# Three 256-column matmuls in the feed-forward part, and weight and activation tiles whose first byte lies at 64 modulo 128

## The chip, the core and the metric

The kernel runs on one core of a Trainium2 chip. The metric is the device time in microseconds (us) of one execution. The median of three runs of the kernel before is 1634.89 us (1634.41 to 1635.89).

The engines are called as the profile calls them: PE is TensorE (its matmuls; PEld are its weight loads), DVE is VectorE, ACT is ScalarE, POOL is GpSimd, SP is SyncE, which issues the DMAs. A matmul has a *stationary* operand of 128x128 values, brought in by a weight load, and a *moving* operand of up to 512 columns that streams past it; sums land in a PSUM bank of 512 f32 columns per partition.

## The reference, cut to what matters

The reference is two transformer-like blocks on 256 tokens of 2048 features, all in float32: a first block with chunk attention and a gated recurrence, a second one with pooling, latent attention, memory attention and a feed-forward part. The change of form touches the feed-forward part:

```python
def conv_glu_ffn(h, w_gate, w_up, conv_w, conv_b, w_down):
    S = h.shape[1]
    g = h @ w_gate                       # [256, 2048] @ [2048, 5632]
    gp = jnp.pad(g, ((0, 0), (CONV_WIDTH - 1, 0), (0, 0)))
    gc = conv_b
    for j in range(CONV_WIDTH):
        gc = gc + conv_w[j] * gp[:, j:j + S]
    return (jax.nn.silu(gc) * (h @ w_up)) @ w_down
```

## The kernel before

**How a product is made.** Every float32 weight product is made of three products of a shorter form (float32r): weights and activations are each split into a high and a low part, and high x high, high x low and low x high are summed in PSUM. `split_w` makes the parts of a half tile of weights (128 partitions x 1024 values): ACT rounds the raw tile `wr` into `wh` (L114), DVE subtracts to get `wl` (L115). `tile_mm` loads one weight tile of 1 MB by a DMA on SP's queue, splits it in two halves and emits the matmuls of each half. Its modes are: `N`, where the activations are stationary and 512 (or 384, or 320) columns of weights move; `T`, where a 128x128 block of weights is stationary and 256 tokens move, with three matmuls for each block (all at L162); and `T2`, for the feed-forward part alone, where the tile of activations holds high and low side by side, so that one matmul of 512 columns (L148) gives high x high and high x low at once, in the two halves of a bank, and one of 256 columns (L149) adds low x high to the first half.

**Stages.** The program runs, in this order: keys and values of the memory (mode N, activations in tiles named `s`), the input projection with modulation beside it (modes N and T, activations `h`), gates (T, `h`), output projection of block 1 (T, activations `yH` and `yL`), input projection of block 2 (N and T, `h`), latent attention (N), output projection of block 2 (T, `yH` and `yL`), and the feed-forward part: for each of 22 column pairs a gate matrix and an up matrix (T2, activations `h`), then 8 column groups of the down matrix (T2, activations `f`). The feed-forward part has 1408 pairs of matmuls on `h` and 704 on `f`.

**What sets the order.** The code is written out once and the order of each engine's queue is that of the code. Evictions are put on a queue of small closures (`later`), and `drain` emits some of them after each half tile, by the table BUDGET; AHEAD says by how many half tiles the splits go ahead of the products (one in gate and up, none in down). In the feed-forward part an eviction of the gate is, for each of two 128-feature blocks, a copy of the second half bank by ACT (L1283), an addition by DVE (L1284) and a product with the token factor by POOL (L1285), then the convolution (L1289 to L1291); of the up matrix a copy (L1311), an addition (L1312), a product (L1313) and a split (L119, L120); of the down matrix two additions (L1334, L1335) and a DMA of the result (L1337).

**Where tiles lie.** SBUF tiles are given out in the order of the code, pool by pool. Adding up their sizes gives these first bytes modulo 128: `wr`, `wh` and `wl` at 32; the tile of `h` at 0; the tiles `yH`, `yL`, `s` and `f` at 96. Steps inside these tiles are multiples of 512 bytes, so every operand of a matmul has the residue of its tile.

Of the kernel before, what the change touches and what calls it, by code (L numbers as in the profile page):

```python
# [26 lines left out]
# PSUM banks for the accumulation of weight products (the others serve everything else)  # L27
MM = 6
# by phase: half tiles by which the splits of the weights go ahead of their products,
# and how much waiting work (microseconds of VectorE) is emitted after each half tile  # L30
AHEAD = dict(mem=0, pass0=0, pass3=1, gz=0, az=1, out=0, in2=1, mla=1, o=0, ffn=1, down=0)
BUDGET = dict(mem=0.3, pass0=0.5, pass3=2.0, gz=1.3, az=1.1, out=0.5, in2=0.1, mla=0.9, o=0.6, ffn=0.1, down=0.3)
# which engine does each of a modulation tile's four chunks, VectorE or ScalarE with GpSimd:
# for the gate's column groups, and for the scale's and the shift's
GATES = ("VVVP", "VVVP", "VVVP", "VVVV")
PAIR = ("PPPP", "VVVV")
# where modulation tiles stand among the projection's column groups, and among the memory's weight tiles
# [3 lines left out]
# stages by which a recurrence pair's transposition follows its last level; costs of the recurrence's steps  # L41
# [17 lines left out]
def trunk_kernel(ctx, tc, a, out):  # L59
# [3 lines left out]
    const = ctx.enter_context(tc.tile_pool(name="const", bufs=1))  # L63
    wpool = ctx.enter_context(tc.tile_pool(name="w", bufs=2))
# [26 lines left out]
    def later(cost, fn, q=None):  # L91
        (bgq if q is None else q).append((cost, fn))

    def drain(budget):
        """Emits waiting work, of about budget microseconds on the vector engine."""
        while budget > 0 and (evq or bgq):
            cost, fn = (evq or bgq).popleft()
            fn()
            budget -= cost
# [24 lines left out]
    def submit(job):  # L124
        """Emits the products of half tiles AHEAD halves behind their splits."""
# [8 lines left out]
    def tile_mm(src, kc0, kt, cw, mode, banks, act, first, last, pre=None, post=None):  # L134
        """One weight tile [kt * P, cw]: banks += weights.T @ activations, transposed (T) or not (N), or transposed
        with a bank for each block, where the low parts of the activations have their own half (T2);
        pre comes before its products, post after them."""
# [4 lines left out]
        def one(kc, b, hi, lo):  # L142
            x = act(kc0 + kc)
            hi, lo = hi[:, kc % nk, :], lo[:, kc % nk, :]
            st, sp = first and kc == 0, last and kc == kt - 1
            if mode == "T2":
                s = slice(b * P, b * P + P)
                PE.matmul(banks[b], hi[:, s], x, start=st, stop=sp, skip_group_check=True)  # L148
                PE.matmul(banks[b][:, :T], lo[:, s], x[:, 0, :], start=False, stop=sp, skip_group_check=True)  # L149
                return  # L150
            xh, xl = x
# [1296 lines left out]
```

## Time and profile before

| what | value |
|---|---|
| median of three runs | 1634.89 us (1634.41 to 1635.89) |
| profiled execution, first to last instruction | 1632.6 us |
| granted clock of PE over the span | 0.993 |
| PE busy | 1569.8 us (96%), 9754 matmuls |
| DVE busy | 1155.7 us (71%) |
| ACT busy | 860.1 us (53%) |
| POOL busy | 378.4 us (23%) |
| moved from HBM | 328 MB, mean 202 GB/s |

The profile is of one execution. Its span lies 2.3 us under the median, which counts what lies ahead of the first instruction and behind the last. Matmuls overlap: the duration of one includes its way through the array, so the time that a stream of them takes is read from the distance of their starts, not from their durations. The view "chain that ended last" follows the run back from its end; a piece such as "2.74 PE mm L162 x24" says that 24 matmuls in a row took 2.74 us of it.

### The profile page before, as it was taken

What the parts mean: (1) busy time and instruction counts of PE and PEld (TensorE: products, weight loads), DVE (VectorE), ACT (ScalarE), POOL (GpSimd) and SP (SyncE); (2) the same over time, 40 slices, a digit from 0 to 9 for tenths busy, and PEclk for the clock granted to TensorE, in tenths of its full rate; (3) what the DMA queues carried; (4) which work ended last, traced back from release to release, by engine and by line L of the source; (5) the groups of instructions that cost most, each with busy time, mean ns of one, the idle gap of its engine ahead of it and who ended that gap; (6) DMA issues with size and microseconds to landing.
All of it is one profiled execution on the core that took longest, in us unless ns stands there. A gap on an engine that the chain in (4) does not pass through costs nothing.

```text
span 1632.6 us, 24896 instructions
## 1 busy us (share of the span) xinstructions
PE 1569.8 (96%) x9754; PEld 1398.2 (86%) x9754; DVE 1155.7 (71%) x1610; ACT 860.1 (53%) x1254; POOL 378.4 (23%) x363
## 2 busy tenths in 40 slices
PE   5789999999899999999999999999999999999999
PEld 4677888978899999888999888888888888888887
DVE  7876998899997778568676666666666666445444
ACT  6466555564556745467455555554555555333332
POOL 3523434056643112513002111111111111000000
PEclk9999999999999999999999999999999999999999
DMA  9568877544665486443445555555555555556553
GB/s 386 224 229 309 329 296 303 181 155 156 214 218 207 155 301 225 160 158 135 147 155 174 188 181 181 186 194 188 181 183 190 192 183 181 187 192 208 193 178 126
DMA packets 50949, 331.75 MB, mean 203 GB/s; under 512 B 5648, under 2 KB 8080, under 8 KB 13456
## 3 DMA queue, kind: packets, MB, share of 16 engines
q1 hardware_dynamic: 50832, 330.17, 56.6%
q8 instruction: 76, 1.25, 0.3%
q14 instruction: 41, 0.34, 0.1%
HBM read 328.05 MB, written 2.10 MB: 202 GB/s over the span
## 4 chain that ended last, share of the span: by engine, by line
PE 83%; DVE 9%; POOL 2%; issue 2%; DMA 2%; ACT 2%; SPq 0%; DVEq 0%; ACTq 0%; POOLq 0%
PE mm L162 32%; PE mm L148 30%; PE mm L149 15%; DVE wl L115 4%; DVE acc L374 1%; PE ax L716 1%; DMA wr<-in_w_mem_kv_dram 1%; ACT wh L114 1%; POOL acc L380 1%; PE ax L389 1%; DMA wr<-in_w_ada_dram 1%; PE ax L250 1%; PE ax L514 1%; DMA yH<-in_w_ada_dram 1%; PE ax L220 0%
## 5 line engine op out<-in xcount | busy, mean ns | idle before, releaser
L115 DVE TENSOR_TENSOR wl<-wr,wh 128x1024 fp32r<-128x1024 f32 (+2 forms) x516 | 666.0, 1293 | 372.3 <-PE mm L149 248.2
L114 ACT CAST wh<-wr 128x1024 fp32r<-128x1024 f32 (+2 forms) x516 | 534.5, 1039 | 493.9 <-PE mm L148 242.0
L148 PE MATMUL mm<-h,wh 128*128 128x512 f32 x1408 | 497.7, 397 | 0.0
L149 PE MATMUL mm<-h,wl 128*128 128x256 f32 x1408 | 396.9, 282 | 0.0
L148 PEld LDWEIGHTS mm<-h,wh 128*128 128x128 f32 x1408 | 264.4, 188 | 64.8
L149 PEld LDWEIGHTS mm<-h,wl 128*128 128x128 f32 x1408 | 266.2, 189 | 0.0
L148 PE MATMUL mm<-f,wh 128*128 128x512 f32 x704 | 248.8, 398 | 0.0
L162 PE MATMUL mm<-wh,h 128*128 128x512 f32 (+1 forms) x704 | 222.4, 391 | 0.0
L162 PE MATMUL mm<-h,wh 128*128 128x256 f32 x1152 | 212.6, 286 | 0.6 <-ACT wh L114 0.6
L149 PE MATMUL mm<-f,wl 128*128 128x256 f32 x704 | 198.1, 281 | 0.0
L162 PEld LDWEIGHTS mm<-h,wh 128*128 128x128 f32 x1152 | 179.6, 191 | 1.6 <-ACT wh L114 1.2
L162 PE MATMUL mm<-h,wl 128*128 128x256 f32 x576 | 164.5, 286 | 7.8 <-DVE wl L115 7.8
L148 PEld LDWEIGHTS mm<-f,wh 128*128 128x128 f32 x704 | 132.6, 188 | 32.7
L162 PEld LDWEIGHTS mm<-wh,h 128*128 128x128 f32 x704 | 131.1, 188 | 27.7
L162 PE MATMUL mm<-wl,h 128*128 128x512 f32 (+1 forms) x352 | 137.1, 389 | 3.3 <-DVE wl L115 3.2
L149 PEld LDWEIGHTS mm<-f,wl 128*128 128x128 f32 x704 | 132.3, 188 | 0.0
L162 PEld LDWEIGHTS mm<-h,wl 128*128 128x128 f32 x576 | 110.1, 191 | 9.9 <-DVE wl L115 9.8
L162 PE MATMUL mm<-yH,wh 128*128 128x256 f32 x512 | 117.5, 282 | 0.0
L162 PE MATMUL mm<-yL,wh 128*128 128x256 f32 x512 | 116.9, 280 | 0.0
L1285 POOL TENSOR_TENSOR gp<-sg,R 128x256 f32<-128x256 f32 x44 | 35.9, 818 | 326.8 <-DVE sg L1284 326.8
L162 PE MATMUL mm<-yH,wl 128*128 128x256 f32 x384 | 106.5, 279 | 2.7 <-DVE wl L115 2.7
L380 POOL TENSOR_TENSOR acc<-acc,pts 128x512 f32<-128x512 f32 x45 | 75.5, 1678 | 112.0 <-ACT pts L379 109.8
(315 smaller groups left out, 2030.1 us busy)
## 6 DMA issues: line engine op xcount, KB each, us to landing
wr<-in_w_in_dram SPq DMA_DIRECT2D x76, 1024.0 KB, 4.9
wr<-in_w_gate_dram SPq DMA_DIRECT2D x44, 1024.0 KB, 4.8
wr<-in_w_up_dram SPq DMA_DIRECT2D x44, 1024.0 KB, 4.9
wr<-in_w_down_dram SPq DMA_DIRECT2D x40, 1024.0 KB, 5.0
yH<-in_w_ada_dram SPq DMA_DIRECT2D x28, 1024.0 KB, 7.1
wr<-in_w_ada_dram SPq DMA_DIRECT2D x16, 1024.0 KB, 5.0
wr<-in_w_out_dram SPq DMA_DIRECT2D x16, 1024.0 KB, 4.9
wr<-in_w_o_dram SPq DMA_DIRECT2D x16, 1024.0 KB, 4.8
```

The source lines that it names most:

```text
L114: S.copy(hi, raw[:, k : k + n, :])
L115: V.tensor_tensor(lo, raw[:, k : k + n, :], hi.bitcast(F32), ALU.subtract)
L148: PE.matmul(banks[b], hi[:, s], x, start=st, stop=sp, skip_group_check=True)
L149: PE.matmul(banks[b][:, :T], lo[:, s], x[:, 0, :], start=False, stop=sp, skip_group_check=True)
L162: PE.matmul(o, l, r, start=st and i == 0, stop=sp and i == 2, skip_group_check=True)
L250: PE.transpose(ps[:, j * T + tb * P : j * T + tb * P + P], d[:, j, tb * P : tb * P + P], ident)
L374: V.scalar_tensor_tensor(accs[0], raw[:, k, :], cc, accs[0], ALU.mult, ALU.add)
L380: G.tensor_tensor(accs[1], accs[1], t, ALU.add)
L389: PE.matmul(ps[:, j * P : j * P + P], acc[:, j * P : j * P + P], ones, start=i == 0, stop=i == len(accs) - 1, skip_group_check=True)
L514: PE.matmul(po[:, :T], vblk(0), t[:, :T], start=True, stop=False, skip_group_check=True)
L716: PE.matmul(ps[:, j, b, :], k2[:, j, s], q2[:, j, s], start=True, stop=True)
L1285: G.tensor_tensor(gp[:, 2:], s, R3, ALU.mult)
```

## The change

In the feed-forward part mode `T2` gives way to mode `T`: three matmuls of 256 columns with 256 columns of output, both blocks of a column pair side by side in one bank. So the evictions work on 512 columns at a time and need no addition of half banks: the gate's is one DVE product with the token factor, straight from PSUM; the up matrix's one DVE product and a split; the down matrix's one DVE addition. Four small tiles of 32 bytes are put ahead of the tiles of four pools (`const`, `h`, `y` and `f`), which moves the first bytes of `wr`, `wh`, `wl`, `h`, `yH`, `yL`, `s` and `f` to 64 modulo 128. The matrices, the DMAs of weights, the splits of weights and the orders of everything else stay.

```diff
@@ trunk_kernel @@
     const = ctx.enter_context(tc.tile_pool(name="const", bufs=1))
+    const.tile([P, 8], F32, tag="pad0", name="pad0")
...
+    hpool.tile([P, 8], F32, tag="pad1", name="pad1")
...
     yp = by.enter_context(tc.tile_pool(name="y", bufs=1))
+    yp.tile([P, 8], F32, tag="pad2", name="pad2")
@@ tile_mm @@
-            x = act(kc0 + kc)
+            xh, xl = act(kc0 + kc)
             hi, lo = hi[:, kc % nk, :], lo[:, kc % nk, :]
             st, sp = first and kc == 0, last and kc == kt - 1
-            if mode == "T2":
-                s = slice(b * P, b * P + P)
-                PE.matmul(banks[b], hi[:, s], x, start=st, stop=sp, skip_group_check=True)
-                PE.matmul(banks[b][:, :T], lo[:, s], x[:, 0, :], start=False, stop=sp, skip_group_check=True)
-                return
-            xh, xl = x
             if mode == "T":
                 o = banks[b // 2][:, (b % 2) * T : (b % 2) * T + T]
                 s = slice(b * P, b * P + P)
                 trip = ((hi[:, s], xh), (hi[:, s], xl), (lo[:, s], xh))
@@ feed-forward @@
         fp = ctx.enter_context(tc.tile_pool(name="f", bufs=1))
+        fp.tile([P, 8], F32, tag="pad2", name="pad2")
...
-    act3 = lambda kc: h3[2][:, :, kc, :]
+    act3 = lambda kc: (h3[0][:, kc, :], h3[1][:, kc, :])
...
-        def start(k, b, gp):
-            G.memset(gp[:, 0:2], 0.0)
-            s = sg[0][:, k, :]
-            S.copy(s, b[:, T:])
-            V.tensor_tensor(s, b[:, :T], s, ALU.add)
-            G.tensor_tensor(gp[:, 2:], s, R3, ALU.mult)
+        def start(b, gp):
+            G.memset(gp[:, :, 0:2], 0.0)
+            V.tensor_tensor(gp[:, :, 2:], two(b), bc(R3, 2), ALU.mult)
...
-            for k, b in enumerate(banks):
-                later(0.4, lambda k=k, b=b: start(k, b, gp[:, k, :]), evq)
+            later(0.8, lambda: start(banks[0], gp), evq)
...
-        def one(k, b):
-            t = tmp([P, T], "ub")
-            S.copy(t, b[:, T:])
-            V.tensor_tensor(t, b[:, :T], t, ALU.add)
-            V.tensor_tensor(t, t, sg[0][:, k, :], ALU.mult)
-            split(t, f[j][:, 0, k, :], f[j][:, 1, k, :])
+        def one(b):
+            t = tmp([P, 2, T], "ub")
+            V.tensor_tensor(t, two(b), sg[0], ALU.mult)
+            split(t, f[j][:, 0], f[j][:, 1])
...
-        linear([(lambda kg: a["w_gate"][j, kg], 256, "T2", ev_gate(j, sg))], range(2), act3, kt=8,
+        linear([(lambda kg: a["w_gate"][j, kg], 256, "T", ev_gate(j, sg))], range(2), act3, kt=8,
                need=lambda kg, j=j: need3(j, kg))
-        linear([(lambda kg: a["w_up"][j, kg], 256, "T2", ev_up(j, sg))], range(2), act3, kt=8)
+        linear([(lambda kg: a["w_up"][j, kg], 256, "T", ev_up(j, sg))], range(2), act3, kt=8)
...
-    actf = lambda kc: f[kc // 2][:, :, kc % 2, :]
+    actf = lambda kc: (f[kc // 2][:, 0, kc % 2, :], f[kc // 2][:, 1, kc % 2, :])
...
-            V.tensor_tensor(x1[:, c, :], b[:, T:], x1[:, c, :], ALU.add)
-            V.tensor_tensor(x1[:, c, :], b[:, :T], x1[:, c, :], ALU.add)
-            if k:
-                SP.dma_start(out[:, c - 1 : c + 1, :], x1[:, c - 1 : c + 1, :])
+            V.tensor_tensor(x1[:, c, :], two(b), x1[:, c, :], ALU.add)
+            SP.dma_start(out[:, c, :], x1[:, c, :])
```

What moves is shown at two places. The first is PE's queue in the feed-forward part, in a gate or up tile on `h3`: before, a bank for each of the two blocks of weights, and two matmuls for each block and chunk.

```order
L149 MATMUL mm_10080<-h3_8453,wl_10104 128x256
L148 MATMUL mm_10079<-h3_8453,wh_10103 128x512
L149 MATMUL mm_10079<-h3_8453,wl_10104 128x256
L148 MATMUL mm_10080<-h3_8453,wh_10103 128x512
L149 MATMUL mm_10080<-h3_8453,wl_10104 128x256
```

The same place after ("x2" is two in a row of the same form: high x high and high x low); the last two rows are those of the next tile, in the next bank.

```order
L156 MATMUL mm_10379<-h3_8456,wl_10467 128x256
L156 MATMUL mm_10379<-h3_8456,wh_10466 128x256 x2
L156 MATMUL mm_10379<-h3_8456,wl_10467 128x256
L156 MATMUL mm_10502<-h3_8456,wh_10498 128x256 x2
L156 MATMUL mm_10502<-h3_8456,wl_10499 128x256
```

Two matmuls of 512 and 256 columns have become three of 256, and one bank takes what two took. The second place is DVE's queue in the feed-forward part, from one gate eviction to the end of the up matrix's: before, additions from PSUM (`mm`) for each block.

```order
L1284 TENSOR_TENSOR sg<-mm,sg 128x256
L1290 SCALAR_TENSOR_TENSOR sg<-gp,cols,sg 128x256
L1291 SCALAR_TENSOR_TENSOR sg<-gp,cols,sg 128x256
L1290 SCALAR_TENSOR_TENSOR sg<-gp,cols,sg 128x256
L115 TENSOR_TENSOR wl<-wr,wh 128x1024
L1291 SCALAR_TENSOR_TENSOR sg<-gp,cols,sg 128x256
L115 TENSOR_TENSOR wl<-wr,wh 128x1024 x2
L1312 TENSOR_TENSOR ub<-mm,ub 128x256
L1313 TENSOR_TENSOR ub<-ub,sg 128x256
L115 TENSOR_TENSOR wl<-wr,wh 128x1024
L120 TENSOR_TENSOR f_8942<-ub,f_8942 128x256
```

The same place after.

```order
L1280 TENSOR_TENSOR gp<-mm,R_8813 128x2x256
L116 TENSOR_TENSOR wl<-wr,wh 128x1024
L1285 SCALAR_TENSOR_TENSOR sg<-gp,cols,sg 128x256 x2
L1286 SCALAR_TENSOR_TENSOR sg<-gp,cols,sg 128x256
L116 TENSOR_TENSOR wl<-wr,wh 128x1024
L1286 SCALAR_TENSOR_TENSOR sg<-gp,cols,sg 128x256
L116 TENSOR_TENSOR wl<-wr,wh 128x1024 x2
L1305 TENSOR_TENSOR ub<-mm,sg 128x512
L116 TENSOR_TENSOR wl<-wr,wh 128x1024
L121 TENSOR_TENSOR f_8981<-ub,f_8981 128x512
```

The token factor's product has come from POOL to DVE, the additions are gone, and the weight splits stand between fewer and longer operations.

## Rows read from the trace of the kernel before

**Rows 1.** The page: span; busy us of each engine (share) xinstructions.

```profile
span 1632.6 us, 24896 instructions
PE 1569.8 (96%) x9754; PEld 1398.2 (86%) x9754; DVE 1155.7 (71%) x1610; ACT 860.1 (53%) x1254; POOL 378.4 (23%) x363
```

**Rows 2.** Busy us by stretches of the feed-forward part: gate and up, then down.

```profile
core 0: us, PE busy (x) PEld busy (x) DVE busy (x) ACT busy (x) POOL busy (x), PEclk, DMA share, GB/s
900.00:1370.00 470.00, 470.00 (x2662) 408.58 (x2661) 311.95 (x415) 245.31 (x355) 78.42 (x100) 1.00 0.53 186
1380.00:1620.00 240.00, 240.00 (x1361) 208.41 (x1360) 116.83 (x117) 90.34 (x88) 0.00 (x0) 1.00 0.56 188
```

**Rows 3.** Chain that ended last: start us, us, what; mode T on `h`.

```profile
419.01 2.84 PE mm L162 x24
511.43 11.36 PE mm L162 x96
```

**Rows 4.** The same chain: mode T on `yH` and `yL`, both output projections.

```profile
538.30 2.73 PE mm L162 x24
578.93 26.21 PE mm L162 x231
...
771.95 5.46 PE mm L162 x48
...
781.58 2.83 PE mm L162 x24
...
817.71 2.83 PE mm L162 x24
...
840.16 21.43 PE mm L162 x188
866.16 14.16 PE mm L162 x118
```

**Rows 5.** The same chain, gate and up: pieces of mode T2 on `h`.

```profile
900.03 0.24 PE mm L148
900.27 0.12 PE mm L149
900.39 0.23 PE mm L148
900.62 0.12 PE mm L149
```

**Rows 6.** Timeline of PE, mode N, 512 columns of weights moving: activations `s`, then `h`.

```profile
55.21 0.39 PE L162 MATMUL mm<-wl,s 128*128 128x512 f32 x1
...
57.95 0.39 PE L162 MATMUL mm<-wl,s 128*128 128x512 f32 x1
...
279.87 0.40 PE L162 MATMUL mm<-wl,h 128*128 128x512 f32 x1
...
282.67 0.40 PE L162 MATMUL mm<-wl,h 128*128 128x512 f32 x1
```

**Rows 7.** Groups of instructions: line engine op, names, shapes, count, busy us, mean ns.

```profile
L162 PE MATMUL mm<-h,wl 128*128 128x256 f32 x576 | 164.5, 286 | 7.8 <-DVE wl L115 7.8
L162 PE MATMUL mm<-wh,h 128*128 128x512 f32 x640 | 206.9, 398 | 0.0
L162 PE MATMUL mm<-wl,h 128*128 128x512 f32 x320 | 127.2, 398 | 3.3 <-DVE wl L115 3.2
```

**Rows 8.** The same view: evictions of the feed-forward part, and one of 512 columns (L1233).

```profile
L1284 DVE TENSOR_TENSOR sg<-mm,sg 128x256 f32<-128x256 f32 x44 | 18.3, 417 | 11.5 <-ACT sg L1283 11.5
L1285 POOL TENSOR_TENSOR gp<-sg,R 128x256 f32<-128x256 f32 x44 | 35.9, 818 | 326.8 <-DVE sg L1284 326.8
L1312 DVE TENSOR_TENSOR ub<-mm,ub 128x256 f32<-128x256 f32 x44 | 18.5, 421 | 11.8 <-ACT ub L1311 11.8
L1313 DVE TENSOR_TENSOR ub<-ub,sg 128x256 f32<-128x256 f32 x44 | 18.7, 426 | 3.0
L1233 DVE TENSOR_TENSOR x<-mm,x 128x512 f32<-128x512 f32 x8 | 5.5, 684 | 0.3
```

**Rows 9.** Timeline of the end.

```profile
1628.30 0.28 PE L149 MATMUL mm<-f,wl 128*128 128x256 f32 x1
...
1628.62 0.42 DVE L1334 TENSOR_TENSOR x<-mm,x 128x256 f32<-128x256 f32 x1 [0.53 <-PE mm L149]
1629.08 0.42 DVE L1335 TENSOR_TENSOR x<-mm,x 128x256 f32<-128x256 f32 x1
1629.53 0.34 SPq L1337 DMA_DIRECT2D out_dram<-x  x1
```

More of the change, by code (lines that the diff above doesn't have):

```diff
@@ L1308, in ev_up @@
     def ev_up(j, sg):
-        def one(k, b):
-            t = tmp([P, T], "ub")
-            S.copy(t, b[:, T:])
-            V.tensor_tensor(t, b[:, :T], t, ALU.add)
-            V.tensor_tensor(t, t, sg[0][:, k, :], ALU.mult)
-            split(t, f[j][:, 0, k, :], f[j][:, 1, k, :])
+        def one(b):
+            t = tmp([P, 2, T], "ub")
+            V.tensor_tensor(t, two(b), sg[0], ALU.mult)
+            split(t, f[j][:, 0], f[j][:, 1])
         def ev(banks):
-            for k, b in enumerate(banks):
-                later(1.0, lambda k=k, b=b: one(k, b), evq)
+            later(1.2, lambda: one(banks[0]), evq)
         return ev
@@ L1322, in trunk_kernel, with one @@
         sg = []
-        linear([(lambda kg: a["w_gate"][j, kg], 256, "T2", ev_gate(j, sg))], range(2), act3, kt=8,
+        linear([(lambda kg: a["w_gate"][j, kg], 256, "T", ev_gate(j, sg))], range(2), act3, kt=8,
                need=lambda kg, j=j: need3(j, kg))
-        linear([(lambda kg: a["w_up"][j, kg], 256, "T2", ev_up(j, sg))], range(2), act3, kt=8)
+        linear([(lambda kg: a["w_up"][j, kg], 256, "T", ev_up(j, sg))], range(2), act3, kt=8)
     finish()
     flush()
-    actf = lambda kc: f[kc // 2][:, :, kc % 2, :]
+    actf = lambda kc: (f[kc // 2][:, 0, kc % 2, :], f[kc // 2][:, 1, kc % 2, :])
     def ev_out(g):
-        def one(k, b):
-            c = 2 * g + k
-            V.tensor_tensor(x1[:, c, :], b[:, T:], x1[:, c, :], ALU.add)
-            V.tensor_tensor(x1[:, c, :], b[:, :T], x1[:, c, :], ALU.add)
-            if k:
-                SP.dma_start(out[:, c - 1 : c + 1, :], x1[:, c - 1 : c + 1, :])
+        def one(b):
+            c = slice(2 * g, 2 * g + 2)
+            V.tensor_tensor(x1[:, c, :], two(b), x1[:, c, :], ALU.add)
+            SP.dma_start(out[:, c, :], x1[:, c, :])
         def ev(banks):
-            for k, b in enumerate(banks):
-                later(0.8, lambda k=k, b=b: one(k, b), evq)
+            later(0.8, lambda: one(banks[0]), evq)
         return ev
@@ L1345, in trunk_kernel @@
     for g in range(8):
-        linear([(lambda kg: a["w_down"][g][:, 2 * kg : min(2 * kg + 2, FC // 4)], 256, "T2", ev_out(g))], range((FC + 7) // 8),
+        linear([(lambda kg: a["w_down"][g][:, 2 * kg : min(2 * kg + 2, FC // 4)], 256, "T", ev_out(g))], range((FC + 7) // 8),
                actf, kt=8, nkc=FC)
```

## The prediction

> **What bounds the kernel now.** I read the page first. PE is busy for 1569.8 of 1632.6 us, DVE for 71% of the span, ACT for 53% [rows 1]. So what counts is how long PE's stream takes, and where PE waits. Then I cut out the feed-forward part: in both stretches PE is busy for the whole window, 470 of 470 us and 240 of 240 us, while DVE has 312 and 117 us of work, ACT 245 and 90, and the DMAs use 53 to 56% of their engines [rows 2]. Nothing but PE sets the end there. The window of 470 us holds 2662 matmuls, or 1331 pairs: 470 / 1331 = 0.3531 us for a pair of 512 and 256 columns; the one of 240 us gives 240 / 680.5 = 0.3527 us. The part has 1408 + 704 = 2112 pairs, so 2112 x 0.353 = 746 us of the run, and every nanosecond on the cost of 768 columns is worth 2.1 us.
>
> What do 768 columns cost elsewhere, in the form that the change brings? The chain shows mode T in two speeds. On `h`, 96 matmuls take 11.36 us, so three take 11.36 / 32 = 0.3550 us, and 24 in another place take the same 0.355 [rows 3]. On `yH` and `yL` it is 26.21 x 3 / 231 = 0.3404 us in the first output projection (and 2.73 / 8 = 0.341 a little earlier), but in the second one 0.341 at 772 us, 2.83 / 8 = 0.354 from 781 to 836 us, 0.342 from 840 us, and 14.16 x 3 / 118 = 0.360 from 866 us [rows 4]. At the clock of these stretches (granted 1.00, which is 2.4 GHz [rows 2]) 768 columns are 0.320 us, so all forms lose something for each column: 0.020 us in the good speed, 0.035 in the middling one, 0.040 in the worst. The loss is not one for each matmul: a pair at 0.3531 loses about what a triple on `h` loses. It shows inside the gate too, where the chain gives 0.24 and 0.23 us by turns to the matmuls of 512 columns [rows 5]: 0.24 against the 0.213 of 512 columns at 2.4 GHz.
>
> What do the speeds go with? The tiles' first bytes modulo 128 are 32 for weights, 0 for `h`, 96 for `yH`, `yL`, `s` and `f`. In mode T the fast stretches have a moving tile at 96 against weights at 32: equal modulo 64. The tile `h` at 0 is not equal to 32 modulo 64, and no piece on it is fast. Mode N says the same the other way round: 12 matmuls of 512 columns take 57.95 - 55.21 = 2.74 us with `s` stationary (96 against 32), 0.2283 each, and 282.67 - 279.87 = 2.80 us with `h` (0 against 32), 0.2333 each [rows 6]. Against it stand the slow stretches of the second output projection, on the same residues, and mode T2 on `f`, at 96 too, with 0.3527. So equal residues modulo 64 look needed for the fast speed, and not sufficient. After the change all of these tiles lie at 64: equal modulo 64 everywhere, but also equal modulo 128, which no stretch of this trace has.
>
> **The change part by part.**
>
> *Pairs to triples, in the fast speed.* 2112 x (0.3404 - 0.3531) = -26.8 us. All of it lies on the path, since PE is never idle there. In the middling speed it is 2112 x (0.3550 - 0.3531) = +4.0 us, in the worst 2112 x (0.360 - 0.3531) = +14.6 us. These are the ends; I take the fast one, because both forms of evidence (modes T and N) are faster where residues are equal modulo 64, and the change makes them so.
>
> *Padding, other stages.* There are 576 triples of mode T on `h` [rows 7]: 576 x (0.3404 - 0.3550) = -8.4 us. Mode N has 640 + 320 = 960 matmuls with `h` [rows 7]: 960 x (0.2283 - 0.2333) = -4.8 us. In those stages DVE and POOL stand on the chain between the matmuls, so part of it turns into longer waits of PE for `wl`; I count half, -4.2 and -2.4 us.
>
> *Evictions.* For a column pair DVE loses two additions of the gate, two of the up matrix and two products (417, 421 and 426 ns), and gets one product and one from PSUM of 512 columns; the nearest row is 684 ns [rows 8]. That is 2.53 us against 1.37. ACT loses its copies, POOL its two products of 818 ns. None of this is on the path as long as DVE has work for two thirds of the time; if that cover were gone the same change would be a gain, not a loss. One bank takes what two took, so PE finds banks free earlier; it does not wait for banks now. The weight splits are not touched.
>
> *The end.* Behind the last matmul two additions of 0.42 us run from 1628.62 to 1629.50 us, then the DMA [rows 9]. One of 0.684 us [rows 8] stands in their place: -0.2 us.
>
> *Transfers.* Weights come by the same DMAs at 186 GB/s [rows 2]; at the fast speed they would have to come 4% faster, with DMA engines busy for a little over half. A raw tile that starts 32 bytes further costs between nothing and what 53% leaves free; I take nothing.
>
> The sum: -26.8 - 4.2 - 2.4 - 0.2 = -33.6 us on a span of 1632.6. The span is 2.3 us below the median; I keep that distance, so 1634.9 - 33.6 = 1601, rounded to 1602 us.
>
> **The rivals.**
>
> *Only the number of matmuls counts, not the padding (slower).* Then a triple costs what it costs on `h` now, 0.355 against 0.3531, in gate, up and down: 2112 x 0.0019 = +4.0 us, -0.2 at the end, 1638.7 us. For it: the pair and the triple are close, whatever the tile, and the second output projection changes its speed with no change of tile. Against it: mode N differs by tile. The Trainium skill, TensorE: Matmul & The Clock Gate, section Back-to-back issue gap, has a time of N / 2.4 + 2.5 ns for one matmul behind another, so three cost one 2.5 ns more than two, 2112 x 2.5 ns = 5.3 us by its figure (an estimate from that page); the trace agrees that the triple on `h` is dearer, with 1.9 ns, but not with the page's total of 0.3275 us for a triple, which no piece reaches.
>
> *Only down gains.* Gate and up stay at the speed of `h`, 1408 x 0.0019 = +2.7 us, and down goes to that of the first output projection, 704 x (0.3404 - 0.3527) = -8.7 us: 1628.7 us. Between this and the forecast lie mixtures such as the second output projection's, fast and slow by turns, around 1618 us.
>
> *Equal residues modulo 128 collide (slower).* Weight loads and moving columns are read at the same time; in the fast stretches they lie 64 bytes apart, in the slow ones on `h` 32 apart, after the change 0 apart. If it is distance that helps, zero is the worst: the 0.360 of the last piece [rows 4] everywhere, which is also what 0.24 for 512 columns makes of 768 [rows 5]. Feed-forward +14.6, mode T on `h` 576 x 0.005 = 2.9, mode N 960 x (0.240 - 0.2333) = 6.4, half of these two, together 19 us: 1654 us. It decides from the point where a triple costs 0.356 us, because 2112 x 0.003 = 6.3 us eat up what the other stages could still gain. For it: distance 64 is the only one with fast stretches. Against it: T2 on `f` has distance 64 as well and is slow. The Trainium skill, SBUF — State Buffer, section Who interferes with whom, gives PE two separate read ports, one for the moving operand and one for the weight load, so by it there is no such collision; the trace has weight loads beside every matmul at 0.3404 and at 0.360 alike, so it doesn't tell.
>
> **How the numbers follow.** Forecast 0.40 at 1602; only down, with the mixtures, 0.13 at 1618 to 1629; only the number counts, 0.20 at 1639; collision 0.27 at 1654. A difference under 0.2% (3.3 us) can't be told from no change. The forecast and nearly all of the second case are faster by more than that: 0.52. Of the third case half falls within it (0.10 with what is left of the second), the other half and the fourth are slower: 0.38. The range: the forecast's own spread runs from 1592 (the halves that I left out of the other stages, and a triple slightly under 0.3404) to 1615; to hold 8 in 10 it must reach through the third case and half of the fourth, to 1652. Below 1592 I leave 0.05, above 1652 0.14.
>
> **What the profile would show.** In the forecast the chain has triples of 0.340 in gate, up and down, 2.74 us for 24 matmuls in the stages on `h`, and 512 columns at 0.228 in mode N. If the padding does nothing, stages on `h` stay at 2.84 us for 24. In a collision, these stages get slower together with the feed-forward part: 24 matmuls at 2.88. The number of DVE's operations falls by 183 rows and its busy time in gate and up by about 22 x 1.2 = 26 us in every case; the end shortens by 0.2 us. The forecast would be wrong at its root if the two speeds of mode T have another cause than where tiles lie, such as a state that PE falls into and keeps; the second output projection is the sign of that.

## The result and the profile after

The changed kernel takes 1652.8 us (median of 4 executions, 1651.21 to 1658.08), the kernel before 1635.39 us beside it (1634.41 to 1637.15): a ratio of 1.0105, 95% interval 1.0088 to 1.0122. It is slower by 1.05%, where 1602 us had been forecast. The profiled execution of it is the one of 1658.08 us, with a span of 1656.2 us.

The page of the changed kernel, span and busy time of each engine (against [rows 1]):

```profile
span 1656.2 us, 28877 instructions
PE 1594.0 (96%) x11866; PEld 1524.5 (92%) x11866; DVE 1121.1 (68%) x1476; ACT 833.0 (50%) x1144; POOL 320.4 (19%) x297
```

PE has 2112 more matmuls and 24.2 us more busy time; DVE, ACT and POOL all have less. So the time lies in PE's stream, not in an engine that feeds it. The same two stretches of the feed-forward part, shifted by 25 us (against [rows 2]):

```profile
core 0: us, PE busy (x) PEld busy (x) DVE busy (x) ACT busy (x) POOL busy (x), PEclk, DMA share, GB/s
925.00:1395.00 470.00, 470.00 (x3919) 470.00 (x3919) 281.63 (x309) 216.02 (x246) 29.14 (x40) 1.00 0.51 183
1405.00:1645.00 240.00, 240.00 (x2002) 240.00 (x2002) 106.83 (x91) 88.35 (x84) 0.00 (x0) 1.00 0.53 184
```

PE is again busy all the time at the same granted clock of 1.00, which is 2.4 GHz. But 470 us hold 3919 matmuls, 1306.3 triples, so 768 columns take 470 x 3 / 3919 = 0.3598 us in gate and up and 240 x 3 / 2002 = 0.3596 us in down; a pair took 0.3531 and 0.3527. PEld, which loads the weights, went from 87% to 100%: there are three loads for 768 columns where there were two. Pieces of the chain that ended last, against [rows 3 and 4] (start us, us, what):

```profile
292.04 10.90 PE mm L156 x48
...
410.62 2.88 PE mm L156 x24
...
513.20 11.51 PE mm L156 x96
...
582.62 20.52 PE mm L156 x171
...
702.98 3.52 PE mm L156 x24
...
710.42 8.22 PE mm L156 x36
...
848.80 23.05 PE mm L156 x192
...
903.75 748.80 PE mm L156 x6240
```

One price stands in all pieces of mode T, whatever the stage: 11.51 / 96 = 0.1199 us for a matmul of 256 columns on `h`, 20.52 / 171 = 0.1200 and 23.05 / 192 = 0.1200 on `yH` and `yL`, and 748.80 / 6240 = 0.1200 in the piece that covers nearly all of the feed-forward part. Before, the stretches on `yH` and `yL` had 0.1135 (26.21 / 231), 0.1140 and, in places, 0.118. The pieces at 292, 703 and 710 us are mode N, with 320 columns (3.52 / 24 = 0.1467) and 512 columns (10.90 / 48 = 0.2271, 8.22 / 36 = 0.2283). 512 columns are faster than before, where they took 0.2333 on `h` [rows 6]; 320 columns are not, the chain before has 3.52 us for 24 as well.

Where did the 23.6 us between the two profiled spans come from? The first matmul of the part on `h`, and the first of down, in the timeline of the kernel before:

```profile
880.16 0.40 PE L148 MATMUL mm<-h,wh 128*128 128x512 f32 x1
...
1379.69 0.39 PE L148 MATMUL mm<-f,wh 128*128 128x512 f32 x1
```

and of the changed one, with its end (against [rows 9]):

```profile
889.85 0.40 PE L156 MATMUL mm<-h,wh 128*128 128x256 f32 x2
...
1398.94 0.40 PE L156 MATMUL mm<-f,wh 128*128 128x256 f32 x2
...
1652.26 0.28 PE L156 MATMUL mm<-f,wl 128*128 128x256 f32 x1
1652.58 0.69 DVE L1325 TENSOR_TENSOR x<-mm,x 128x512 f32<-128x512 f32 x1 [4.47 <-PE mm L156]
1653.29 0.34 SPq L1326 DMA_DIRECT2D out_dram<-x  x1
```

Ahead of the feed-forward part 889.85 - 880.16 = +9.7 us; gate and up 509.1 against 499.5 us, +9.6; down (to DVE's last eviction) 253.6 against 248.9, +4.7; behind that -0.4. The two middle terms are the triple's price: 1408 x (0.3598 - 0.3531) = 9.4 and 704 x (0.3596 - 0.3527) = 4.9. The first term is partly this execution's own: it is 5.3 us above the median of its kernel, and t_all32 below, which has the same distances between all tiles, begins its long piece 3.4 us earlier (900.34 against 903.75). The rest of it was not taken apart.

The evictions did what the diff says (against [rows 8]: four kinds of work on 256 columns became two on 512):

```profile
L1280 DVE TENSOR_TENSOR gp<-mm,R 128x512 f32<-128x512 f32 x22 | 15.2, 692 | 33.6 <-PE mm L156 33.6
L1305 DVE TENSOR_TENSOR ub<-mm,sg 128x512 f32<-128x512 f32 x22 | 15.2, 692 | 36.4 <-PE mm L156 36.4
```

Both wait for PE, not PE for them. This saving, some 30 us of DVE in the first stretch (311.95 against 281.63), is worth nothing here, where PE is busy all the time.

### The profile page after: what moved, and what is told of

The parts are those of the page before. It is cut to its first block, busy times and chain, and to the rows that moved or that the text cites. A ratio compares the mean times of both kernels' runs of the same rounds, so it can differ in the third digit from the quotient of the medians.

```text
span 1656.2 us, 28877 instructions
## 1 busy us (share of the span) xinstructions
PE 1594.0 (96%) x11866; PEld 1524.5 (92%) x11866; DVE 1121.1 (68%) x1476; ACT 833.0 (50%) x1144; POOL 320.4 (19%) x297
## 4 chain that ended last, share of the span: by engine, by line
PE 83%; DVE 8%; DMA 2%; POOL 2%; ACT 2%; issue 2%; SPq 0%; DVEq 0%; ACTq 0%; POOLq 0%
PE mm L156 78%; DVE wl L116 3%; DVE acc L371 1%; PE ax L713 1%; ACT wh L115 1%; DMA wr<-in_w_mem_kv_dram 1%; POOL acc L377 1%; PE ax L214 1%; PE ax L244 1%; DMA yH<-in_w_ada_dram 1%; PE ax L511 1%; PE ax L386 1%; DMA wr<-in_w_out_dram 0%; DVE yH L714 0%; PE ax L503 0%
## 5 line engine op out<-in xcount | busy, mean ns | idle before, releaser
L116 DVE TENSOR_TENSOR wl<-wr,wh 128x1024 fp32r<-128x1024 f32 (+2 forms) x516 | 679.2, 1318 | 381.6 <-PE mm L156 336.2
L156 PE MATMUL mm<-h,wh 128*128 128x256 f32 x3968 | 721.9, 285 | 0.4 <-ACT wh L115 0.4
L156 PEld LDWEIGHTS mm<-h,wh 128*128 128x128 f32 x3968 | 621.3, 193 | 1.4 <-ACT wh L115 1.0
L156 PEld LDWEIGHTS mm<-h,wl 128*128 128x128 f32 x1984 | 381.9, 193 | 9.7 <-DVE wl L116 9.4
L156 PE MATMUL mm<-f,wh 128*128 128x256 f32 x1408 | 253.5, 283 | 0.0
L156 PEld LDWEIGHTS mm<-f,wh 128*128 128x128 f32 x1408 | 219.8, 192 | 0.0
L156 PEld LDWEIGHTS mm<-wh,h 128*128 128x128 f32 x704 | 131.2, 188 | 24.2
L156 PEld LDWEIGHTS mm<-yH,wh 128*128 128x128 f32 x512 | 89.5, 193 | 2.4 <-ACT wh L115 2.4
L156 PEld LDWEIGHTS mm<-yL,wh 128*128 128x128 f32 x512 | 89.4, 193 | 0.0
L156 PEld LDWEIGHTS mm<-wl,h 128*128 128x128 f32 x352 | 66.2, 188 | 18.6 <-DVE wl L116 6.9
L156 PEld LDWEIGHTS mm<-yH,wl 128*128 128x128 f32 x384 | 74.0, 193 | 1.4 <-DVE wl L116 1.4
```

Source lines behind the costliest of these rows:

```text
L116: V.tensor_tensor(lo, raw[:, k : k + n, :], hi.bitcast(F32), ALU.subtract)
L156: PE.matmul(o, l, r, start=st and i == 0, stop=sp and i == 2, skip_group_check=True)
```

## The experiments

The change has two halves, so the first two runs make one each. After that the subject is where tiles lie. The places below are first bytes modulo 256, from the built programs; every tile steps by multiples of 512 bytes, so the place holds for all of its slices. d is the place of the activation tile less that of the weight tile, modulo 256. Before: weights at 32, `h` at 0 (d = 224), `y` tiles and `f` at 224 (d = 192). After: all at 64, d = 0. A run's name gives places modulo 128, as the prediction used them. All runs have the triples (mode T) except pair_at_64. The others differ from the changed kernel in pad tiles alone, but for the edits of `spread` that two of the later sections show. Where only one execution was timed, the text says "one execution".

**t_unpadded: the triples without the padding.**

```
-    const.tile([P, 8], F32, tag="pad0", name="pad0")
-    hpool.tile([P, 8], F32, tag="pad1", name="pad1")
-    yp.tile([P, 8], F32, tag="pad2", name="pad2")
-        fp.tile([P, 8], F32, tag="pad2", name="pad2")
```

> The change of form alone: three 256-column matmuls in the feed-forward part, without the padding (weights at 32 modulo 128, h at 0, yH, yL and f at 96). Theory 'distance' (what counts is the distance modulo 128 between the moving and the stationary tile: 0 is worst, 64 best, 32 between): gate and up keep 0.355 us for a triple (distance 32), down gets 0.340 to 0.354 (distance 64), and the stages before the feed-forward part stay as they are: 1629 to 1638 us. Rival 'form' (the three matmuls themselves cost the 0.360, the padding nothing): 0.360 everywhere in the feed-forward part, 1650 us.

1627.88 us (1625.86 to 1629.49), a ratio of 0.9945, interval 0.9928 to 0.9962: faster than before. Two windows inside gate and up, and inside down:

```profile
925.00:1370.00 445.00, 445.00 (x3763) 445.00 (x3762) 270.93 (x292) 206.28 (x234) 26.88 (x38) 1.00 0.53 185
1410.00:1600.00 190.00, 190.00 (x1679) 190.00 (x1678) 89.54 (x78) 73.47 (x70) 0.00 (x0) 1.00 0.60 208
```

A triple takes 445 x 3 / 3763 = 0.3548 us on `h`, and 190 x 3 / 1679 = 0.3395 us on `f`. This is the prediction's case "only down gains" (1628.7 us), by its own two prices. So the form alone is a gain.

**pair_at_64: the padding without the triples** (the kernel before with the pads).

```
+    const.tile([P, 8], F32, tag="pad0", name="pad0")
+    hpool.tile([P, 8], F32, tag="pad1", name="pad1")
+    yp.tile([P, 8], F32, tag="pad2", name="pad2")
+        fp.tile([P, 8], F32, tag="pad3", name="pad3")
```

> The padding alone: the pair of 512 and 256 columns stays, all weight and activation tiles at 64 modulo 128 (distance 0). Theory 'distance': the stages in mode T before the feed-forward part have 0.360 for a triple as in the changed kernel, and the pair in the feed-forward part goes to 0.24 + 0.12 = 0.360 as well: about 1652 us. Rival 'triples only' (distance 0 hurts only where a weight load runs beside every 256 columns): the pair stays at 0.353 or goes down towards 0.227 + 0.120 = 0.347, and the run ends between 1625 and 1640 us.

1624.4 us (1623.01 to 1626.55), a ratio of 0.9929, interval 0.9906 to 0.9953. The padding alone is a gain too. The first of the same windows:

```profile
925.00:1370.00 445.00, 445.00 (x2569) 392.36 (x2569) 303.06 (x401) 237.84 (x342) 74.05 (x99) 1.00 0.54 189
```

A pair takes 445 x 2 / 2569 = 0.3464 us against 0.3531, as the rival of the expectation has it. So the two halves gain 0.55% and 0.7% alone and lose 1.05% together. That is no sum of two effects, and one price accounts for it: with d = 0 every matmul, whatever its columns, loses the same 13 ns over its columns at 2.4 GHz. 256 columns: 0.1200 - 0.1067 = 13.3 ns. 320: 0.1467 - 0.1333 = 13.4 ns. 512: 0.2271 - 0.2133 = 13.8 ns (15.0 in the dearest of the three pieces). A pair is 320 + 2 x 13.2 ns, a triple 320 + 3 x 13.3 = 360 ns. At the places of before a pair lost 33 ns and a triple on `h` 35 ns: about the same, so the number of matmuls did not show. The padding made the loss one for each matmul, which helps whoever has few and long ones (mode N and T2) and hurts mode T; the other half of the change turned two matmuls into three.

**t_w64_h0_y32_f96 and t_w0_h0_y64_f32: different places for each tile.** Weights, `h`, `y`, `f` at 64, 128, 160, 96 (d = 64, 96, 32) and at 128, 128, 192, 160 (d = 0, 64, 32).

```
# t_w64_h0_y32_f96
-    hpool.tile([P, 8], F32, tag="pad1", name="pad1")
+    hpool.tile([P, 24], F32, tag="pad1", name="pad1")
-    yp.tile([P, 8], F32, tag="pad2", name="pad2")
+    yp.tile([P, 16], F32, tag="pad2", name="pad2")
-        fp.tile([P, 8], F32, tag="pad2", name="pad2")
# t_w0_h0_y64_f32
-    const.tile([P, 8], F32, tag="pad0", name="pad0")
+    const.tile([P, 24], F32, tag="pad0", name="pad0")
-    yp.tile([P, 8], F32, tag="pad2", name="pad2")
+    yp.tile([P, 24], F32, tag="pad2", name="pad2")
-        fp.tile([P, 8], F32, tag="pad2", name="pad2")
+        fp.tile([P, 16], F32, tag="pad3", name="pad3")
```

> Triples, weights at 64 modulo 128, h at 0 (distance 64), yH, yL and s at 32 (distance 32 below), f at 96 (distance 32 above). Theory 'distance': triples on h, so gate and up, at 0.340; output projections and down at 0.355; time about 1634.9 - 18 (gate, up) + 1.3 (down) - 4 (other stages on h) + 4 (output projections) = 1618 us. Rival 'residue' (what counts is where the activations lie by themselves, with 0 giving 0.355 and 96 giving 0.340): h stays at 0.355, f at 0.340.

> Triples, weights at 0 modulo 128, h at 0 (distance 0), yH, yL and s at 64 (distance 64), f at 32 (distance 32). Theory 'distance': h, gate and up at 0.360, output projections at 0.340, down at 0.355; about 1640 to 1645 us. Rival 'residue' (a tile at 64 is slow by itself): output projections at 0.360 and h at 0.355 as before.

1644.38 and 1645.6 us, one execution each. From the first kernel's chain a piece on `yH` and `yL` (d = 96), then its two windows:

```profile
844.48 23.04 PE mm L156 x192
```

```profile
925.00:1370.00 445.00, 445.00 (x3780) 445.00 (x3779) 273.36 (x294) 207.90 (x236) 28.05 (x39) 1.00 0.53 187
1410.00:1600.00 190.00, 190.00 (x1586) 190.00 (x1584) 84.44 (x72) 69.45 (x66) 0.00 (x0) 1.00 0.56 192
```

and the second kernel's long piece:

```profile
895.89 744.12 PE mm L156 x6240
```

In the first, a matmul on `yH` and `yL` (d = 96) takes 23.04 / 192 = 0.1200 us, one on `h` (d = 64) 445 / 3780 = 0.1177 us and one on `f` (d = 32) 190 / 1586 = 0.1198. In the second, `h` is at d = 0 again, at another place than after (128 for 64). With 0.1200 on its 4128 matmuls, the rest of the piece is (744.12 - 4128 x 0.1200) / 2112 = 0.1178 us for `f`, at d = 32 again. So d = 0 costs 0.1200 elsewhere too, but at d = 32 two kernels differ: d alone does not settle it. For the first kernel neither expectation holds: 'distance' fails on `h` (0.3532 us for a triple where it has 0.340), 'residue' on `f` (0.3594 where it has 0.340).

**t_w32_act96, t_w96_act32, t_all32: distance 64 or distance 0.** All activations at 96 with weights at 32, then weights at 96 and activations at 160 (d = 64 both), then all at 32 (d = 0).

```
# t_w32_act96
-    const.tile([P, 8], F32, tag="pad0", name="pad0")
-    hpool.tile([P, 8], F32, tag="pad1", name="pad1")
+    hpool.tile([P, 24], F32, tag="pad1", name="pad1")
# t_w96_act32
-    const.tile([P, 8], F32, tag="pad0", name="pad0")
+    const.tile([P, 16], F32, tag="pad0", name="pad0")
-    hpool.tile([P, 8], F32, tag="pad1", name="pad1")
+    hpool.tile([P, 24], F32, tag="pad1", name="pad1")
# t_all32
-    const.tile([P, 8], F32, tag="pad0", name="pad0")
```

> Triples; weights at 32 modulo 128, all activations (h, yH, yL, s, f) at 96: distance 64, the residues at which down took 0.340 us for a triple in t_unpadded. Theory 'load stall' (a weight load whose tile has the residue of the moving tile costs a fixed 13.3 ns, whatever the columns; at distance 64 with both at 32 modulo 64 it is half of that): triples at 0.340 in gate, up, down and all stages in mode T, 512 columns in mode N at 0.230: 1634.9 - 2112 x 0.013 - 576 x 0.015 - 960 x 0.004 = 1595 us. Rival 'state' (the 113 and 118 ns are states into which PE falls, tiles have no say in it): gate and up stay at 0.355, and the run at t_unpadded's 1628 us.

> Triples; the mirror of t_w32_act96: weights at 96, all activations at 32. Theory 'load stall', if the distance alone counts: the same as t_w32_act96, triples at 0.340. Rival: it matters which of the two lies in the upper half of 128 bytes; then triples at 0.350 or above.

> Triples; weights and all activations at 32 modulo 128: distance 0 once more, but neither at a multiple of 64. Theory 'load stall': 0.360 for a triple and 0.2267 for 512 columns in mode N, exactly as at 64 and at 0, so about 1652 us. Rival 'multiples of 64 are slow': triples between 0.340 and 0.354.

t_w32_act96: 1638.47 us (1636.85 to 1641.63), a ratio of 1.0008, interval 0.9997 to 1.0019; t_w96_act32 1638.58 and t_all32 1654.68 us, one execution each. The long pieces, in this order:

```profile
897.85 734.94 PE mm L155 x6240
```

```profile
898.11 734.94 PE mm L156 x6240
```

```profile
900.34 748.80 PE mm L155 x6240
```

The two kernels with d = 64 take 734.94 / 6240 = 0.1178 us for a matmul, to the same hundredth of a microsecond over the whole piece; the kernel with d = 0 takes 748.80, as the changed one does. Places moved by 32 or 64 bytes with d kept change nothing here. In these long streams d = 64 is not fast, in none of the ten executions of t_w32_act96: equal places modulo 64, which all three kernels have, are not enough for the 0.1135 that the prediction took from them. But d = 64 has fast streams too. Earlier in the trace of t_w96_act32, on `h`, with the same distance:

```profile
245.45 0.28 PE L156 MATMUL mm<-h,wl 128*128 128x256 f32 x1
...
259.05 0.28 PE L156 MATMUL mm<-h,wl 128*128 128x256 f32 x1
```

40 triples lie between these two, 13.60 / 40 = 0.340 us each, or 0.1133 for a matmul. The traces with d = 0 have no stream of mode T at that speed.

**t_d192 and t_d128: the modulus.** In the kernel before, `y` and `f` have d = 192, which modulo 128 can't be told from 64. t_d192 gives all activations that distance (224), t_d128 puts them at 160, so at 0 modulo 128 but 128 modulo 256.

```
# t_d192
-    const.tile([P, 8], F32, tag="pad0", name="pad0")
-    hpool.tile([P, 8], F32, tag="pad1", name="pad1")
+    hpool.tile([P, 56], F32, tag="pad1", name="pad1")
# t_d128: the same with
+    hpool.tile([P, 40], F32, tag="pad1", name="pad1")
```

> Triples; weights at 32 modulo 256, all of h, yH, yL, s and f at 224, 192 bytes apart. t_w32_act96 and t_w96_act32 had a distance of 64 modulo 256 and 117.8 ns a matmul; down in t_unpadded had 192 and 113.3 ns. Theory 'distance modulo 256': triples at 0.340 in gate, up, down and the other stages in mode T, 512 columns in mode N at 0.230: about 1595 to 1600 us. Rival 'modulo 128' (64 and 192 are the same): 0.353 and 1638 us as t_w32_act96, or the fast and slow stretches of the kernel before by turns, near 1615 us.

> Triples; weights at 32 modulo 256, activations at 160, 128 bytes apart: distance 0 modulo 128, but not modulo 256. Theory 'distance modulo 256': something other than the 0.360 for a triple and 0.2267 for 512 columns in mode N. Rival 'modulo 128': 0.360 and 0.2267 as in t_all32, about 1653 us.

t_d128: 1644.56 us, one execution.

```profile
898.49 740.49 PE mm L155 x6240
```

740.49 / 6240 = 0.1187 us: not the 0.1200 of d = 0, so 0 and 128 are not the same distance and the modulus is not 128. That rests on one execution, 6.7 us below the fastest one of the changed kernel, and short streams of it take 0.1200 too (2.88 us for 24 at 455 us). Whether the modulus is 256 or more, no run tells. And 64 and 192 have the same two prices, 0.1133 and 0.1178, so nothing here tells these two apart. t_d192: 1631.27 us (1629.95 to 1640.02), a ratio of 0.9975, interval 0.9961 to 0.9989, far from the 1604 that 0.1133 throughout would give; it is slow and fast by turns, as the rival of its expectation allows. Its timeline at the first matmuls of the feed-forward part shows why (the matmul of L226 is the one with which `spread` fills R):

```profile
888.36 0.28 PE L155 MATMUL mm<-h,wl 128*128 128x256 f32 x1
...
890.06 0.28 PE L155 MATMUL mm<-h,wl 128*128 128x256 f32 x1
890.18 0.59 PE L226 MATMUL ax<-R,ones 128*128 128x256 f32 x2
...
890.84 0.28 PE L155 MATMUL mm<-h,wl 128*128 128x256 f32 x1
...
892.61 0.28 PE L155 MATMUL mm<-h,wl 128*128 128x256 f32 x1
```

Each triple has one matmul on `wl`. Five triples take 890.06 - 888.36 = 1.70 us ahead of L226, 0.340 each, and 892.61 - 890.84 = 1.77 us behind it, 0.354 each. Tiles, engines and clock are the same. And behind it the speed stays: the long piece of this chain is

```profile
890.77 734.95 PE mm L155 x6240
```

0.1178 us for each of 6240 matmuls. So at d = 192 a stream has two speeds, and they changed at one short interruption.

**t_d192_split and t_d192_eight: another interruption.** The matmul of `spread` cut in two; or eight more of 128 columns behind it.

```
# t_d192_split, against t_d192
-            PE.matmul(ps, ones, flat(dg), start=True, stop=True)
+            for tb in range(2):
+                PE.matmul(ps[:, tb * P : tb * P + P], ones, dg[:, tb, :], start=True, stop=True, skip_group_check=True)
# t_d192_eight, against t_d192, behind S.copy(R, ps)
+            more = bank("ax")
+            for i in range(8):
+                PE.matmul(more[:, 0:P], ones, dg[:, i % 2, :], start=i == 0, stop=i == 7, skip_group_check=True)
```

> The tiles of t_d192 (weights at 32, activations at 224 modulo 256), with one edit: the single fp32 matmul of 256 columns with which `spread` fills R, in the middle of the feed-forward stream, becomes two of 128 columns, one for each token block. In t_d192 the triples took 0.340 us up to that matmul and 0.353 for the 735 us behind it. Theory (two speeds at this distance; which one holds is set when the stream of float32r matmuls starts again after an interruption, and kept): the restart is changed, so the stream may leave it in the fast speed; then all of gate, up and down run at 0.340 and the run takes 1631.3 - 2112 x 0.0133 = about 1604 us; if it leaves in the slow speed again, 1631. Rival (the loss grows on its own with time or with the stage, whatever interrupts): 0.353 from about the same place, 1631.

> As t_d192, with eight more fp32 matmuls of 128 columns behind the one of `spread` (their result isn't read), so that the stream of float32r matmuls starts again behind a row like that of token_R's sixteen, after which it was fast. The eight cost about 8 x 0.109 = 0.9 us. Theory (speed set at the restart): 0.340 behind it, about 1604 us; in the slow speed 1632. Rival (the loss comes whatever interrupts): 1632. If of this kernel and t_d192_split one is fast and the other slow, the restart decides.

The times of each kernel fall in two groups: t_d192_split took 1602.54, 1602.8 and 1604.94 us, and once 1630.79 us; t_d192_eight four times 1604.93 to 1607.51 and six times 1632.52 to 1635.27 us. The kernel before took 1635.85 us beside them (1632.12 to 1638.53). The faster group of t_d192_split has a ratio of 0.9804 to it, interval 0.9781 to 0.9827. The long piece of t_d192_split:

```profile
892.18 707.23 PE mm L155 x6240
```

707.23 us where t_d192 has 734.95 for the same 6240 matmuls: 0.1133 against 0.1178 us. The difference, 27.7 us, is the one between the groups. In the trace of t_d192_eight the stream switched the other way:

```profile
889.25 0.28 PE L155 MATMUL mm<-h,wl 128*128 128x256 f32 x1
...
891.37 0.28 PE L155 MATMUL mm<-h,wl 128*128 128x256 f32 x1
891.49 0.59 PE L226 MATMUL ax<-R,ones 128*128 128x256 f32 x2
891.92 1.95 PE L230 MATMUL ax<-R,ones 128*128 128x128 f32 x16
...
894.30 0.28 PE L155 MATMUL mm<-h,wl 128*128 128x256 f32 x1
...
894.98 0.28 PE L155 MATMUL mm<-h,wl 128*128 128x256 f32 x1
```

Six triples at 2.12 / 6 = 0.353 us ahead, 0.68 / 2 = 0.340 behind, and that for the rest of the run (707.24 us for 6240). The eight took 1.95 us, not the 0.9 that I had expected of them. That the loss grows by itself, with time or stage, is refuted; that the restart after an interruption decides the speed, and the stream keeps it, fits both traces. What in the restart decides is not shown; it is not the program alone, since executions of one program fall in both groups.

**t_d160 and t_act224_wl96: is another distance always fast, and does each load pay for itself?** Activations at 192 (d = 160); and t_d192_split with `wl` moved to 96, so that d is 192 for the loads of `wh` and 128 for those of `wl`.

```
# t_d160
-    const.tile([P, 8], F32, tag="pad0", name="pad0")
-    hpool.tile([P, 8], F32, tag="pad1", name="pad1")
+    hpool.tile([P, 48], F32, tag="pad1", name="pad1")
-        fp.tile([P, 8], F32, tag="pad2", name="pad2")
+        fp.tile([P, 72], F32, tag="pad3", name="pad3")
# t_act224_wl96, against t_d192_split
+        if not padw:
+            padw.append(wpool.tile([P, 16], F32, tag="padw", name="padw", bufs=1))
-    hpool.tile([P, 56], F32, tag="pad1", name="pad1")
+    hpool.tile([P, 40], F32, tag="pad1", name="pad1")
```

> As t_d192, with all activation tiles at 192 modulo 256, so 160 behind the weights at 32: the one multiple of 32 that no run has had. Its neighbours are 192 (113.3 or 117.8 ns for 256 columns, one or the other for a whole stream) and 128 (118.7 ns). Theory (192 alone is special, the only distance at which a stream can run at 113): 118 to 119 ns, triples of 0.355, about 1640 us. Rival (the fast speed belongs to a band of distances below 192, and 160 lies in its middle): 113 ns in every stream, triples of 0.340, about 1604 us in all executions.

> As t_d192_split, with the low parts of the weights 64 bytes further (96 modulo 256), the high parts still at 32 and the activations at 224: distance 192 for two of a triple's loads, 128 for the third. Theory (each load's own distance counts, and the speed of a stream is kept by all of its loads): no stream can hold the fast speed, since the load of wl breaks it in every triple; 0.353 to 0.356 for a triple, 1631 to 1638 us in all executions. Rival (each load pays for itself, with no memory): two fast loads and one of 118.7, triples of 0.345, about 1614 us.

t_d160: 1645.11 us (1643.42 to 1653.26), a ratio of 1.0057, interval 1.0038 to 1.0077. t_act224_wl96: 1640.95 us (1639.39 to 1644.84), 1.0028, 1.0016 to 1.0040. Pieces of their chains, with the long ones last:

```profile
513.39 11.39 PE mm L155 x96
...
786.08 2.82 PE mm L155 x24
...
898.92 748.81 PE mm L155 x6240
```

```profile
581.29 20.23 PE mm L159 x171
...
898.17 737.72 PE mm L159 x6240
```

There is no band of fast places around d = 160. Its profiled execution, the one of 1653.26 us, pays 0.1200 for each matmul of the long stream, the price of d = 0; the other five are 8 to 10 us faster. The trace shows that d = 160 has several speeds too: 11.39 / 96 = 0.1186 and 2.82 / 24 = 0.1175 us stand in it beside 0.1200, so the faster executions can be those whose long stream took one of these; none of them was profiled. And with one load of three at another distance the fast speed is gone from the whole stream: 737.72 x 3 / 6240 = 0.3547 us for a triple, where two fast loads and one at d = 128 paying each for itself would give 0.345, and nine executions within 5.5 us with none near 1604. It is gone from the other stages of this trace too: 20.23 / 171 = 0.1183 us in the first output projection, where t_d192 has 26.21 us for 231, 0.1135.

**t_act32_wl96: `wl` at another distance than `wh`.** It was meant to have distance 0 for two loads of three, and by places modulo 128, in which its expectation is written, it has. Modulo 256 it has not: the 64 bytes ahead of `wl` move the activations as well, and with the 96 and 32 bytes of the other pads they lie at 160. So d is 128 for the two loads of `wh` (at 32) and 64 for that of `wl` (at 96), and no load of this kernel has d = 0.

```
# against t_all32
+        if not padw:
+            padw.append(wpool.tile([P, 16], F32, tag="padw", name="padw", bufs=1))
-    hpool.tile([P, 8], F32, tag="pad1", name="pad1")
+    hpool.tile([P, 24], F32, tag="pad1", name="pad1")
```

> Triples; wh and all activations at 32 modulo 128, wl alone at 96. A triple loads wh, wh, wl. While the first matmul runs wh is loaded for the second, while the second runs wl is loaded for the third, while the third runs wh is loaded for the next triple. Theory 'load stall': the stall falls on the matmul beside whose moving columns the load runs, so the second of each triple is the short one, 0.113 to 0.118 us against 0.120 for the other two: 0.353 to 0.358 for a triple. Rival (the stall goes with the stationary tile that is in use): the third is the short one. Rival 'state': no pattern by tile, all three alike.

1622.65 us, one execution, with 1637.36 us for the kernel before beside it.

```profile
510.85 11.20 PE mm L159 x96
...
522.27 2.87 PE mm L159 x24
...
896.03 721.09 PE mm L159 x6240
```

A triple of the long piece takes 721.09 x 3 / 6240 = 0.3467 us. It lies below the 0.353 to 0.358 that had been expected, and below what these distances cost in the long pieces of other kernels, load by load: 2 x 0.1187 + 0.1178 = 0.3552. So the prices of the loads do not add up here either. Nor is 0.3467 the price of the place: earlier streams of the same trace take 11.20 / 96 = 0.1167 and 2.87 / 24 = 0.1196 us for a matmul, against 0.1156. On which of the three matmuls the loss falls is left open, and how load and stream get into each other's way is not settled.

## Why the prediction was wrong

- **The step that failed** is the choice of the fast end, 0.3404 us, out of three that the prediction had worked out, on the ground that "the change makes them so" (equal modulo 64). It put tiles that are 0 apart together with tiles that are 64 or 192 apart, and only the latter had fast stretches. At d = 0 triples cost 0.3598. The term of -26.8 us was 2112 x (0.3598 - 0.3531) = +14 us. The term of -4.2 had the wrong sign as well (mode T on `h` went from 0.1183 to 0.1200 for a matmul), and mode T on `yH` and `yL`, which the sum took as unchanged, went from 0.1135 to 0.1200 where it had been fast. Only the term for mode N had its sign right. The rule as it was worded, needed and not sufficient, is not refuted: every fast stream shown here has d = 64 or 192. But t_w32_act96 (0.1178) and t_all32 (0.1200) show how far from sufficient it is. The prediction itself says that no stretch of its trace has distance 0; it was an extrapolation with no row behind it.
- **The collision, the rival at 0.27, is what happened**: 0.360 for a triple, 2.88 us for 24 matmuls on `h`, 1654 us against the measured 1652.8. Its word for it (distance zero is the worst) holds for 256 columns in so far as no distance was slower; 96 was as slow. Its price was luck. The 0.360 "from 866 us" is not the speed of a stream. The piece holds one late matmul, the first behind a wait, and the others run near the middling speed, as the timeline before shows:

```profile
866.16 0.39 PE L162 MATMUL mm<-yL,wl 128*128 128x256 f32 x1 [1.14 <-DVE wl L115]
866.39 0.40 PE L162 MATMUL mm<-yL,wh 128*128 128x256 f32 x2
...
880.05 0.28 PE L162 MATMUL mm<-yH,wl 128*128 128x256 f32 x1
```

The first takes 0.23 us to the next start, the 116 steps from there to the last (880.05 - 866.39) / 116 = 0.1178. So the worst of the three speeds, 0.040 us of loss, stood in no stream of mode T before. The rival's price for mode N does not hold either. It put 512 columns at 0.240, from the gate's 0.24 [rows 5], which belongs to d = 224; they got faster, to 0.227 or 0.228, as a loss of one for each matmul makes them. It also left out mode T on `yH` and `yL`. These two errors have opposite signs, and its sum came out near by that.

- **"The loss is not one for each matmul"** was right for the places before (33 ns for a pair, 35 for a triple) and was taken over to the new ones, where the loss is one for each matmul (26 and 40 ns). That is why each half gains alone and both lose together.
- **"Only down gains"**, 1628.7 us, is what t_unpadded does, 1627.88 us: the prices of the form at the old places were read rightly, those of the padding were not. The forecast's own time is reached too: t_d192_split takes 1603.87 us in the median, with the triple at 0.340. The fast speed was there to be had, at another distance.
- **A state that PE keeps**, named as the thing that would make the forecast wrong at its root, exists at d = 192 (and 64), and its two prices are those of the stretches of the second output projection (d = 192) that go fast and slow by turns. So the prediction had named the right sign. It was not the cause here: at d = 0 all stages have one price.
- **Evictions, end, transfers**: all as told, and small. DVE has 30 us less to do in the first stretch (26 predicted) and PE did not notice; the end is -0.2 us, 0.71 from DVE's last operation to the DMA against 0.91 [rows 9]; DMA engines are busy for 51 and 53% against 53 and 56%. DVE lost 134 operations (1610 - 1476), not 183. The sum gives 1601.3 us, so 1602 is a slip of rounding, which changes nothing.
- **What the page said of it.** A triple of down takes 0.3395 us in t_unpadded and 0.3596 in the changed kernel, at the same clock, with the same loads and columns; the two programs differ in pad tiles alone. The Trainium skill, SBUF — State Buffer, section Who interferes with whom, gives PE two independent read ports, one for the moving operand and one for the weight load, from which one would expect that distance does not matter. Here the measurement decides: it does. Which port or buffer causes it, no run tells.

## What to carry to other kernels

When a stream of weight loads and matmuls bounds a kernel, divide its busy time by its matmuls, compare that with columns over the granted clock, and ask whether the loss goes with the matmul or with the column before changing their number: here form and padding each gained and together lost by that. Do not take a piece's time over its count for the speed of a stream before its first matmuls have been looked at. Where tiles lie modulo 256 bytes is a parameter like any other; try the form at several distances (pad tiles are cheap), time several executions of each, since one distance can have more than one speed, and never infer a place's speed from another place. Of what ran here, pair_at_64 (1624.4 us) is faster than both kernels in every execution; t_d192_split (1603.87 us) is the fastest, 2% below the kernel before in three executions of four, and in the fourth 0.3%.

## What the runs showed of the hardware that I had not expected

- A float32r matmul with a weight load beside it costs 113.3 to 120.0 ns for 256 columns (106.7 at 2.4 GHz), by the distance of the two tiles' first bytes: d = 0 120.0; 32 117.8 in one kernel, 119.8 in another; 64 and 192 113.3 or 117.8; 96 120.0; 128 118.7 in the long stream; 160 117.5, 118.6 or 120.0, by the stream; 224 118.3.
- At d = 0 the loss is about the same for each matmul, 13.3 ns at 256 columns, 13.4 at 320 and 13.8 to 15.0 at 512.
- At d = 192 the speed is taken at the restart after an interruption as short as one matmul and kept for up to 735 us. It is worth 27.7 us of this kernel, it changes in either direction, and not the same way in every execution of one program.
- With one load of three at another distance (128 where the others have 192) no stream was fast (0.3547 against 0.340 us for a triple).
